# Row halves in three blocks of the output projection, and a shorter reduction at the end

## The chip, the cores and the metric

The kernel runs on one NeuronCore of a Trainium2 chip. The metric is device microseconds of one execution; the median of several executions is compared. The engines are called by the names of the profile: PE (TensorE, the matrix engine; PEld is its weight load), DVE (VectorE), ACT (ScalarE), POOL (GpSimd) and SP (SyncE, which issues most DMAs here).

## The reference

One block of a model with two branches, for 256 tokens of width 2048, with 256 context tokens beside them. The tokens are normalised and modulated, projected into many columns, go through a gated linear recurrence (16 heads) and a windowed attention (16 heads), and are merged. The change lies in the very last part:

```python
y = sigmoid(m_a + b_m[0]) * (hg_branch @ w_o_hgrn) + sigmoid(m_b + b_m[1]) * (att_branch @ w_o_attn)
h = h + gate * (y @ w_out)              # y: 256 x 2048, w_out: 2048 x 2048, gate: one row of 2048
return rmsnorm(h, final_norm_gain)      # h * rsqrt(mean(h*h) + 1e-6) * gain
```

All of it is in float32.

## The kernel before

**Products.** Every matrix is held as two parts, a high one rounded to the engine's float32r type and a low one, the rest. A product of a 128 x 128 block of activations and a 128 x 512 block of weights is three matmuls into the same bank of PSUM (`mm3`, lines 83 to 85): high x high, high x low, low x high. In the output projection the activations (`XH`, `XL`, by `y_st`) are the stationary operand, loaded by LDWEIGHTS, and the weights stream as the moving operand. The tile of activations is called `xHL` in the profile.

**Weights.** `wload` (line 66) issues the DMA of a chunk of 512 KB into one of four buffers `raw`. `wchunk` splits it: ACT copies it rounded into `wh` (line 76), DVE subtracts to get `wl` (line 77). Each of `wh` and `wl` has three buffers. Both instructions have a high priority for the scheduler, so they go ahead of other work that is ready.

**Blocks.** `proj_tok` computes 512 output columns for both token tiles (t = 0 and 1, 128 tokens each). It takes one bank for each token tile with `bank()`, from the pool `pj` of four banks, and walks over the 2048 rows of the weights two blocks of 128 at a time: a chunk gives 2 x 2 x 3 = 12 matmuls, and a block has 16 x 2 x 3 = 96. So one block uses two banks while the two of the block before are read out.

**Order.** In this stage the order of each engine is set when the program is built, by a scheduler that simulates the engines and takes the ready instruction of the highest priority. It can move products ahead of others that aren't ready yet. Semaphores keep the data right on the chip.

**The end of the kernel.** `part_b(3)`, with the last transposes of `y` (line 1061, tile `tky`) and their split, comes ahead of the output projection. Three blocks of 512 columns follow (n = 0, 1, 2), each with `settle` for both token tiles: on DVE `ht` = product x gate (line 1087) and `xv` += `ht` (line 1088), on ACT the squares and their sum (line 1091), on DVE the multiplication by the final gain (line 1096). The last 512 columns come as two pieces of 256. The first goes like a block, in chunks of 512 rows by 256 columns. For the second, all chunks are split into `bH` and `bL` (lines 884 and 885 are the lines of `split`), and its products run for token tile 0 and then for token tile 1, so that tile 0's output is finished while TensorE works on tile 1. For each tile then: `settle` of the last piece, with the squares on DVE (line 1093), a small DVE instruction that adds the sums of the other pieces (line 1127), the power -0.5 on POOL (line 1128), the scaling on ACT and DVE (lines 1132, 1135, 1137), and the output DMAs (line 1139).

Of the kernel before, what the change touches and what calls it, by code (L numbers as in the profile page):

```python
# [7 lines left out]
F32 = mybir.dt.float32  # L8
F32R = mybir.dt.float32r
U8 = mybir.dt.uint8  # L10
AF = mybir.ActivationFunctionType
ALU = mybir.AluOpType
PSUM = bass.MemoryType.PSUM

P = 128
D = 2048
T = 256
KT = D // P
# [20 lines left out]
def block_kernel(ctx: ExitStack, tc: tile.TileContext, x, c, cx, c_ctx, w_ada, b_ada, norm_gain, w_in,  # L39
                 b_merge, lb_f, lb_b, hg_gain, w_oh, sink, w_oa, w_out, fin_gain, cst, msk, out):  # L40
    nc = tc.nc
    pe, act, dve, pool = nc.tensor, nc.scalar, nc.vector, nc.gpsimd

    def pl(name, bufs=1, **kw):
        return tc.tile_pool(name=name, bufs=bufs, **kw)
# [5 lines left out]
    base = ctx.enter_context(pl("base"))  # L51
# [9 lines left out]
    def wload(w, row0, nk, col0, ncol, rp=None):  # L61

        raw = (rp or wp).tile([P, 1024], F32, tag="raw", name="raw", bufs=8 if rp else 4)
        rv = raw[:, : len(col0) * nk * ncol].rearrange("p (g k c) -> p g k c", g=len(col0), k=nk)
        for g, co in enumerate(col0):
            nc.sync.dma_start(rv[:, g], w[row0: row0 + nk * P, co: co + ncol].rearrange("(k p) c -> p k c", p=P))
        return raw, rv

    def wchunk(w, row0, nk, col0, ncol):
        cl = col0 if isinstance(col0, tuple) else (col0,)  # L70
        raw, rv = wload(w, row0, nk, cl, ncol)
        h = wp.tile([P, 1024], F32R, tag="wh", name="wh", bufs=3)
        lo = wp.tile([P, 1024], F32R, tag="wl", name="wl", bufs=3)
        n = len(cl) * nk * ncol
        with tc.high_priority(PRIO):
            act.activation(h[:, :n], raw[:, :n], AF.Copy)  # L76
            dve.tensor_tensor(lo[:, :n], raw[:, :n], h[:, :n].bitcast(F32), op=ALU.subtract)  # L77
        parts = [(h[:, g * nk * ncol: (g + 1) * nk * ncol].rearrange("p (k c) -> p k c", k=nk),
                  lo[:, g * nk * ncol: (g + 1) * nk * ncol].rearrange("p (k c) -> p k c", k=nk)) for g in range(len(cl))]
        return parts if isinstance(col0, tuple) else parts[0]  # L80

    def mm3(o, s, m, first, last):
        pe.matmul(o, s[0], m[0], start=first, stop=False)  # L83
        pe.matmul(o, s[0], m[1], start=False, stop=False)  # L84
        pe.matmul(o, s[1], m[0], start=False, stop=last)  # L85

    def bank(name="pj"):
        return pj.tile([P, 512], F32, tag="pj", name=name)

    def proj_tok_g(w, col0, src, toks):  # L90


        banks = [bank() for _ in toks]
        for k0 in range(0, KT, 2):
            h, lo = wchunk(w, k0 * P, 2, col0, 512)
            for i, t in enumerate(toks):
                for j in range(2):
                    mm3(banks[i], src(k0 + j, t), (h[:, j, :], lo[:, j, :]), k0 + j == 0, k0 + j == KT - 1)
            yield len(toks) * 6 * 512
        return banks  # L100

    def result(g):

        while True:
            try:
                next(g)
            except StopIteration as e:
                return e.value

    def proj_tok(*a):  # L110
        return result(proj_tok_g(*a))
# [109 lines left out]
    with pl("st", reuse_waits="tile") as st:  # L221
        cT = st.tile([P, KT, 32], F32, name="cT")
        mod = st.tile([P, 2, KT, 2], F32, name="mod")
        rows = st.tile([48, P], F32, name="rows")
# [8 lines left out]
        rv = lambda a: a.rearrange("(r p) -> r p", p=P)  # L233
# [649 lines left out]
    def split(dh, dl, src, **kw):  # L883
        act.activation(dh, src, AF.Copy, **kw)
        dve.tensor_tensor(dl, src, dh.bitcast(F32), op=ALU.subtract)
# [11 lines left out]
    with tc.manual_schedule(engines={mybir.EngineType.PE}):  # L897
# [25 lines left out]
        for t in range(4):  # L923
            rows = slice(8 + 2 * t, 10 + 2 * t)
# [120 lines left out]
    xv = [at.tile([P, D], F32, tag=tg, name="xv") for tg in ("A", "X2")]  # L1045
    fg = [at.tile([P, 1024], F32, tag=tg, name="fg") for tg in Q_TAGS[0]]
    gt = [at.tile([P, 1024], F32, tag=tg, name="gt") for tg in Q_TAGS[1]]
# [27 lines left out]
    def y_st(kt, t):  # L1075
        sl = slice(t * P, (t + 1) * P)
        return XH[:, kt, sl], XL[:, kt, sl]

    fin = few.tile([P, 16], F32, name="fin")
    ssf = fin[:, :10].rearrange("p (t n) -> p t n", t=2)  # L1080
    rsf = fin[:, 10:12]
    def settle(t, bo, c0, width, slot, gain=True):

        cl = slice(c0, c0 + width)
        ch = slice(c0 % 1024, c0 % 1024 + width)
        ht = base.tile([P, 512], F32, tag="bb", name="ht", bufs=2)[:, :width]
        dve.tensor_tensor(ht, bo, gt[c0 // 1024][:, ch], op=ALU.mult)
        dve.tensor_tensor(xv[t][:, cl], xv[t][:, cl], ht, op=ALU.add)
        sq = base.tile([P, 512], F32, tag="sm", name="fsq", bufs=3)[:, :width]
        if gain:  # L1090
            act.activation(sq, xv[t][:, cl], AF.Square, accum_out=ssf[:, t, slot: slot + 1])
        else:
            dve.scalar_tensor_tensor(sq, xv[t][:, cl], 1.0, xv[t][:, cl], op0=ALU.mult, op1=ALU.mult,
                                     accum_out=ssf[:, t, slot: slot + 1])
        if gain:
            dve.tensor_tensor(xv[t][:, cl], xv[t][:, cl], fg[c0 // 1024][:, ch], op=ALU.mult)

    for n in range(3):
        bo = proj_tok(w_out, n * 512, y_st, range(2))
        for t in range(2):  # L1100
            settle(t, bo[t], n * 512, 512, n)

    bo = [bank() for _ in range(2)]
# [5 lines left out]
    for k0 in range(0, KT, 4):  # L1109
        raw, _ = wload(w_out, k0 * P, 4, (D - 256,), 256)  # L1110
        rv = raw.rearrange("p (k c) -> p k c", k=4)
        ks = slice(k0, k0 + 4)
        with tc.high_priority(PRIO):
            split(bH[:, ks, :], bL[:, ks, :], rv)
    for t in range(2):
        settle(t, bo[t][:, :256], D - 512, 256, 3)

        tot = fin[:, 12 + t: 13 + t]
        dve.tensor_reduce(tot, ssf[:, t, 0:4], mybir.AxisListType.X, ALU.add)
        dve.tensor_scalar(tot, tot, 1.0 / D, EPS, op0=ALU.mult, op1=ALU.add)  # L1120
    for t in range(2):
        be = bank()
        for kt in range(KT):
            mm3(be[:, :256], y_st(kt, t), (bH[:, kt, :], bL[:, kt, :]), kt == 0, kt == KT - 1)
        settle(t, be[:, :256], D - 256, 256, 4, False)
        rs = rsf[:, t: t + 1]
        dve.tensor_scalar(rs, ssf[:, t, 4:5], 1.0 / D, fin[:, 12 + t: 13 + t], op0=ALU.mult, op1=ALU.add)
        pool.tensor_tensor(rs, rs, mhalf[:, :1], op=ALU.pow)
        for c0, c1, on_act in ((0, 512, True), (512, 1024, False), (1024, 1536, True), (1536, D, False)):
            o_ = xv[t][:, c0: c1]  # L1130
            if on_act:
                act.activation(o_, o_, AF.Copy, scale=rs)
            else:
                e = min(c1, D - 256)
                dve.tensor_scalar(xv[t][:, c0: e], xv[t][:, c0: e], rs, None, op0=ALU.mult)
                if e < c1:
                    dve.scalar_tensor_tensor(xv[t][:, e: c1], xv[t][:, e: c1], rs, fg[1][:, e - 1024: c1 - 1024],
                                             op0=ALU.mult, op1=ALU.mult)
            (nc.scalar if on_act else nc.sync).dma_start(out[t * P: (t + 1) * P, c0: c1], o_)
# [53 lines left out]
```

## Time and profile before

| what | value |
|---|---|
| median of 3 runs | 1636.76 us (1636.32 to 1637.85) |
| the profiled execution's own time | 1636.14 us |
| span of the profile, first to last instruction | 1634.3 us |
| PE, DVE, ACT busy | 99%, 57%, 47% of the span |
| mean granted PE clock | 0.997 |
| output projection, blocks of 512 columns | about 1537 to 1603 us |
| output projection, pieces of 256 columns | 1603 to 1626 us |
| behind the last matmul | 1626.3 to 1634.3 us |

Times in rows of the timeline are microseconds from the start of the span: first the start, then the duration, then engine, line, operation, and output<-inputs. `128*128` is the part of the array that a matmul uses, rows x columns, and `128x512` what it writes or streams. A row with `x2` at its end merges neighbours of one kind. Matmuls overlap in the array, so the duration of one is its latency; what a stream of them costs is read from the distance of their starts. In rows that group instructions, the numbers after the bar are the total busy time in us, the mean of one in ns, and the idle time before them with what ended it. Some matmul records are missing from a trace.

### The profile page before, as it was taken

How to read it: one execution, taken by the hardware profiler on the slowest of the kernel's cores; microseconds unless marked ns; L12 is line 12 of the kernel's file. 1: busy time of each engine (PE TensorE's matmuls, PEld its weight loads, DVE VectorE, ACT ScalarE, POOL GpSimd, SP SyncE). 2: the span in 40 equal slices, each digit the busy share in tenths (PEclk: the TensorE clock that was granted, in tenths of full speed). 3: DMA queues.
4: the chain of work that ended last, by engine and by line, in shares of the span. 5: the costliest groups of instructions: out<-in, count | busy, mean ns of one | idle time of the engine just before them, and what ended most of it. 6: DMA issues, size and time to landing. Idle time of an engine off the chain costs nothing.

```text
span 1634.3 us, 24809 instructions
## 1 busy us (share of the span) xinstructions
PE 1613.9 (99%) x9882; PEld 1329.3 (81%) x9882; DVE 937.0 (57%) x1463; ACT 763.4 (47%) x1200; POOL 31.4 (2%) x88
## 2 busy tenths in 40 slices
PE   7999999999999999999999999999999999999998
PEld 4558888888888888888888888888888888788887
DVE  4444467536665466645567455235677676555565
ACT  4333454424553345433566443224576787454443
POOL 2000000000000000000000000000000000000000
PEclk9999999999999999999999999999999999999999
DMA  9993444336343453435335555424544454665554
GB/s 356 383 384 109 142 150 149 110 127 195 104 129 117 156 176 106 131 117 177 118 119 176 186 193 193 129 90 142 179 140 146 133 168 157 231 201 192 184 191 140
DMA packets 191427, 274.89 MB, mean 168 GB/s; under 512 B 9776, under 2 KB 112592, under 8 KB 190544
## 3 DMA queue, kind: packets, MB, share of 16 engines
q1 hardware_dynamic: 189344, 268.95, 50.1%
q0 software_dynamic: 1248, 3.25, 0.7%
q8 instruction: 77, 1.26, 0.3%
q10 hardware_dynamic: 720, 1.11, 0.2%
q14 instruction: 38, 0.31, 0.1%
HBM read 271.17 MB, written 2.11 MB: 167 GB/s over the span
## 4 chain that ended last, share of the span: by engine, by line
PE 95%; DMA 2%; DVE 1%; issue 1%; ACT 0%; SPq 0%; POOLq 0%; POOL 0%; ACTq 0%
PE pj L83 24%; PE pj L85 23%; PE pj L84 23%; PE pj L141 7%; PE pj L146 4%; DMA raw<-in_w_ada_dram 2%; PE pa L306 2%; PE al L562 1%; PE pj L396 1%; PE pj L389 1%; PE sb L643 1%; PE tkp L1001 1%; PE pj L390 1%; PE oba L83 0%; PE sc L85 0%
## 5 line engine op out<-in xcount | busy, mean ns | idle before, releaser
L77 DVE TENSOR_TENSOR wl<-raw,wh 128x1024 fp32r<-128x1024 f32 x392 | 479.6, 1224 | 425.4 <-ACT wh L76 425.0
L76 ACT ACTIVATE wh<-raw 128x1024 fp32r<-128x1024 f32 x392 | 414.7, 1058 | 589.4 <-PE pj L85 428.6
L84 PE MATMUL pj<-wl,xHL 128*128 128x512 f32 (+1 forms) x1024 | 395.6, 386 | 0.4 <-DVE wl L77 0.4
L85 PE MATMUL pj<-wh,xHL 128*128 128x512 f32 (+1 forms) x1024 | 395.4, 386 | 0.0
L83 PE MATMUL pj<-wh,xHL 128*128 128x512 f32 (+1 forms) x1024 | 391.4, 390 | 0.0
L85 PEld LDWEIGHTS pj<-wh,xHL 128*128 128x128 f32 x1024 | 192.4, 188 | 39.0
L84 PEld LDWEIGHTS pj<-wl,xHL 128*128 128x128 f32 x1024 | 192.5, 188 | 38.2 <-DVE wl L77 0.7
L83 PEld LDWEIGHTS pj<-wh,xHL 128*128 128x128 f32 x1024 | 192.2, 188 | 37.8 <-DVE yt L1057 0.4
L141 PE MATMUL pj<-xHL,wh 128*128 128x512 f32 x512 | 181.1, 396 | 0.0
L83 PE MATMUL pj<-xHL,wh 128*128 128x512 f32 x416 | 164.6, 396 | 0.0
L85 PE MATMUL pj<-xHL,wl 128*128 128x512 f32 x416 | 162.1, 390 | 0.0
L84 PE MATMUL pj<-xHL,wh 128*128 128x512 f32 x416 | 162.0, 389 | 0.0
L146 PE MATMUL pj<-xHL,wl 128*128 128x256 f32 x512 | 139.9, 283 | 0.0
L141 PEld LDWEIGHTS pj<-xHL,wh 128*128 128x128 f32 x512 | 95.0, 188 | 19.2
L84 PE MATMUL pj<-wl,bH 128*128 128x512 f32 x256 | 99.9, 390 | 0.0
L85 PE MATMUL pj<-wh,bL 128*128 128x512 f32 x256 | 99.6, 389 | 0.0
L146 PEld LDWEIGHTS pj<-xHL,wl 128*128 128x128 f32 x512 | 96.7, 189 | 2.5
L85 PEld LDWEIGHTS pj<-xHL,wl 128*128 128x128 f32 x416 | 78.1, 188 | 16.7
L83 PEld LDWEIGHTS pj<-xHL,wh 128*128 128x128 f32 x416 | 78.1, 188 | 15.5
L84 PEld LDWEIGHTS pj<-xHL,wh 128*128 128x128 f32 x416 | 78.2, 188 | 15.4
L83 PE MATMUL pj<-wh,bH 128*128 128x512 f32 x256 | 89.8, 390 | 0.1
L608 DVE TENSOR_TENSOR A<-A,X 128x512 f32<-128x512 f32 x96 | 62.0, 687 | 16.7 <-ACT qk L538 6.7
(278 smaller groups left out, 1688.2 us busy)
## 6 DMA issues: line engine op xcount, KB each, us to landing
raw<-in_w_in_dram SPq DMA_DIRECT2D x292, 512.0 KB, 3.5
raw<-in_w_ada_dram SPq DMA_DIRECT2D x128, 256.0 KB, 5.5
raw<-in_w_ada_dram SPq DMA_DIRECT2D x32, 512.0 KB, 3.7
raw<-in_w_o_hgrn_dram SPq DMA_DIRECT2D x32, 512.0 KB, 3.5
raw<-in_w_o_attn_dram SPq DMA_DIRECT2D x32, 512.0 KB, 3.7
raw<-in_w_out_dram SPq DMA_DIRECT2D x32, 512.0 KB, 4.3
raw<-in_w_in_dram SPq DMA_DIRECT2D x24, 256.0 KB, 5.5
X<-in_x_dram SPq DMA_DIRECT2D x2, 1024.0 KB, 6.7
```

The costliest lines, as they stand in the source:

```text
L76: act.activation(h[:, :n], raw[:, :n], AF.Copy)
L77: dve.tensor_tensor(lo[:, :n], raw[:, :n], h[:, :n].bitcast(F32), op=ALU.subtract)
L83: pe.matmul(o, s[0], m[0], start=first, stop=False)
L84: pe.matmul(o, s[0], m[1], start=False, stop=False)
L85: pe.matmul(o, s[1], m[0], start=False, stop=last)
L141: pe.matmul(banks[i].rearrange("p (a t) -> p a t", a=2), h[:, j, cs_], xHL[:, :, kt, :T], start=kt == 0, stop=kt == KT - 1)
L146: pe.matmul(banks[i][:, :T], lo[:, j, cs_], xH[:, kt, :T], start=False, stop=False)
L306: pe.matmul(pa[32 * g: 32 * g + 32, : 2 * w], cT[:, k0 + g, :], rv_[:, :, g % nk, :], start=k0 == 0, stop=k0 == KT - 4, tile_position=(0, ...
L389: pe.matmul(o, hw, xH[:, kt, :], start=kt == 0, stop=False)
L390: pe.matmul(o, lo[:, kt - k, cs_], xH[:, kt, :], start=False, stop=False)
L396: pe.matmul(o, hw, xL[:, kt, :], start=False, stop=kt == KT - 1)
L608: dve.tensor_tensor(av, av, f.unsqueeze(3).to_broadcast([P, 2, n2, b]), op=ALU.mult)
```

## The change

Three edits, all behind `part_b`.

- In the three blocks of 512 columns, `proj_tok` is replaced by the new `in_rows`. It takes four banks, two for each token tile. Each of the three matmuls of a product becomes two: one over the upper 64 rows of the array (partitions 0 to 63 of both operands) into one bank, one over the lower 64 rows into the other. At the end of the block ACT copies the second bank into SBUF and DVE adds the first.
- In the last 256 columns the gate is multiplied into the weights, four times 128 x 1024 on DVE before the split, in place of a multiplication of each product.
- In the last chain of each token tile the product is added to `xv` straight from PSUM, and the squares, their sum, the factor 1/D and the sum of the other pieces are one DVE instruction.

```diff
-    def settle(t, bo, c0, width, slot, gain=True):
+    def settle(t, bo, c0, width, slot):
...
-        if gain:
-            act.activation(sq, xv[t][:, cl], AF.Square, accum_out=ssf[:, t, slot: slot + 1])
-        else:
-            dve.scalar_tensor_tensor(sq, xv[t][:, cl], 1.0, xv[t][:, cl], op0=ALU.mult, op1=ALU.mult,
-                                     accum_out=ssf[:, t, slot: slot + 1])
-        if gain:
-            dve.tensor_tensor(xv[t][:, cl], xv[t][:, cl], fg[c0 // 1024][:, ch], op=ALU.mult)
+        act.activation(sq, xv[t][:, cl], AF.Square, accum_out=ssf[:, t, slot: slot + 1])
+        dve.tensor_tensor(xv[t][:, cl], xv[t][:, cl], fg[c0 // 1024][:, ch], op=ALU.mult)
+
+    def in_rows(col0):
+
+        banks = [[bank(), bank()] for _ in range(2)]
+        for k0 in range(0, KT, 2):
+            m = wchunk(w_out, k0 * P, 2, col0, 512)
+            for t in range(2):
+                for j in range(2):
+                    s = y_st(k0 + j, t)
+                    for n_, (a, b) in enumerate(((0, 0), (0, 1), (1, 0))):
+                        for r in range(2):
+                            rows = slice(64 * r, 64 * r + 64)
+                            pe.matmul(banks[t][r], s[a][rows], m[b][rows, j, :], start=k0 + j + n_ == 0,
+                                      stop=k0 + j == KT - 1 and n_ == 2, tile_position=(64 * r, 0))
+        out_ = []
+        for t in range(2):
+            o = base.tile([P, 512], F32, tag="sm", name="rsum", bufs=3)
+            act.activation(o, banks[t][1], AF.Copy)
+            dve.tensor_tensor(o, banks[t][0], o, op=ALU.add)
+            out_.append(o)
+        return out_
 
     for n in range(3):
-        bo = proj_tok(w_out, n * 512, y_st, range(2))
+        bo = in_rows(n * 512)
         for t in range(2):
             settle(t, bo[t], n * 512, 512, n)
...
         with tc.high_priority(PRIO):
+
+            dve.tensor_tensor(rv, rv, gt[1][:, 768:].unsqueeze(1).to_broadcast([P, 4, 256]), op=ALU.mult)
             split(bH[:, ks, :], bL[:, ks, :], rv)
...
-        settle(t, be[:, :256], D - 256, 256, 4, False)
         rs = rsf[:, t: t + 1]
-        dve.tensor_scalar(rs, ssf[:, t, 4:5], 1.0 / D, fin[:, 12 + t: 13 + t], op0=ALU.mult, op1=ALU.add)
+        xe = xv[t][:, D - 256:]
+        dve.tensor_tensor(xe, xe, be[:, :256], op=ALU.add)
+        sq = base.tile([P, 512], F32, tag="sm", name="fsq", bufs=3)[:, :256]
+        dve.tensor_tensor_reduce(sq, xe, xe, 1.0 / D, fin[:, 12 + t: 13 + t], op0=ALU.mult, op1=ALU.add, accum_out=rs)
         pool.tensor_tensor(rs, rs, mhalf[:, :1], op=ALU.pow)
```

## The prediction

> **What bounds the kernel now.** I read the page first (busy shares and the chain that ended last), then the windows over the output projection, then the timeline of single engines at the places that the diff touches.
>
> ```profile
> span 1634.3 us, 24809 instructions
> ...
> PE 1613.9 (99%) x9882; PEld 1329.3 (81%) x9882; DVE 937.0 (57%) x1463; ACT 763.4 (47%) x1200; POOL 31.4 (2%) x88
> ...
> PE 95%; DMA 2%; DVE 1%; issue 1%; ACT 0%; SPq 0%; POOLq 0%; POOL 0%; ACTq 0%
> ```
>
> TensorE is busy 99% of the span and carries 95% of the chain: a product that gets cheaper or dearer moves the end by the same amount, unless TensorE then waits. The windows show the output projection:
>
> ```profile
> 1537.00:1603.00 66.00, 66.00 (x297) 54.62 (x296) 39.62 (x43) 29.23 (x34) 0.00 (x0) 1.00 0.57 190
> 1603.00:1616.50 13.50, 13.50 (x114) 13.46 (x113) 10.54 (x13) 7.36 (x10) 0.00 (x0) 1.00 0.38 122
> ```
>
> The columns are the window, its length, then busy time of PE, PEld, DVE, ACT and POOL, granted clock, DMA share and GB/s. The first row holds the three quarters that the change rewrites (about 288 products and 8 transposes): TensorE has no idle time at full granted clock, and DVE and ACT have 26 and 37 us to spare. In the second, the first half of the last quarter, DVE is already busy 10.54 of 13.50 us.
>
> Next is the price of a product. The first two rows stand 12 products of 512 columns apart, the last two 45 products of 256 columns:
>
> ```profile
> 1578.64 0.62 PE L83 MATMUL pj<-wh,xHL 128*128 128x512 f32 x2
> ...
> 1581.36 0.62 PE L83 MATMUL pj<-wh,xHL 128*128 128x512 f32 x2
> ...
> 1620.63 0.28 PE L85 MATMUL pj<-bH,xHL 128*128 128x256 f32 x1
> ...
> 1626.03 0.28 PE L85 MATMUL pj<-bH,xHL 128*128 128x256 f32 x1
> ```
>
> 2.72 / 12 = 226.7 ns and 5.40 / 45 = 120.0 ns. The difference of 106.7 ns over 256 columns is 0.417 ns a column, so 512 columns stream in 213.4 ns and each product carries 13.3 ns beside the streaming. That 13.3 ns is all that halves running together can take away.
>
> **The change part by part. The halves (term A).** 3 x 16 x 2 x 3 = 288 products become 576 matmuls of 64 rows, each still streaming 512 columns. If two halves run together with nothing beside the streaming, a pair costs 213.4 ns: 288 x -13.3 = -3.8 us. If they run one after the other it costs 2 x 226.7: +65.3 us. No row of this trace shows row halves. The nearest are tiles of 32 array columns, against the same kind of matmul untiled:
>
> ```profile
> 234.02 0.39 PE L85 MATMUL pj<-xHL,wl 128*128 128x512 f32 x1
> 234.34 0.46 PE L562 MATMUL al<-Kmt 128*32 128x32 f32 x32
> ...
> 235.21 0.65 PE L562 MATMUL al<-so,acc 128*32 128x64 f32 x32
> 235.80 0.66 PE L669 MATMUL kt<-cs,A 128*128 128x128 f32 x4
> ...
> 245.69 0.39 PE L702 MATMUL ob<-so,A 128*128 128x128 f32 x2
> ...
> 246.36 0.39 PE L702 MATMUL ob<-so,A 128*128 128x128 f32 x2
> ```
>
> Untiled, six matmuls of 128 columns lie between the last two rows: 112 ns each, 0.87 ns a column, so 64 columns would take some 56 ns. The 32 tiled ones of 64 columns start within 0.65 - 0.22 = 0.43 us (0.22 us is one's latency), 14 ns each, so four take 56 ns: four column tiles run in the time of one, and their weight loads with them. I carry that over to row halves, with the weight loads as the doubt:
>
> ```profile
> L84 PEld LDWEIGHTS pj<-wl,xHL 128*128 128x128 f32 x1024 | 192.5, 188 | 38.2 <-DVE wl L77 0.7
> ...
> L562 PEld LDWEIGHTS al<-acc,Kmt 128*32 128x32 f32 x256 | 3.1, 108 | 0.0
> ...
> L1061 PEld LDWEIGHTS tky<-cs,y 128*128 128x128 f32 x32 | 4.0, 139 | 1.0
> ...
> L1061 PE MATMUL tky<-cs,y 128*128 128x128 f32 x32 | 4.8, 272 | 0.0
> ...
> 1542.77 0.60 PE L1061 MATMUL tky<-cs,y 128*128 128x128 f32 x4
> ...
> L349 PEld LDWEIGHTS tp<-cs,rows 80*128 80x128 f32 x1 | 0.1, 143 | 0.0
> ```
>
> A load goes by columns: 188 - 108 = 80 ns for 96 more is 0.83 ns a column, 107 ns for 128; and 80 rows (143 ns) cost what 128 rows do (139 ns, the same operation). So a half's load is no cheaper, and a pair has two: 2 x 107 = 213 ns if they take turns, just what the streaming takes. The closest that matmuls with a load of 128 columns each stand in this trace is 109 ns (the four transposes at 1542.77: 0.60 less one's 0.27 leaves 0.33 for three) to 120 ns (the 256-column products), so taking turns gives 218 to 240 ns. I take 219 ns, between 213.4 and the first of these: 288 x -7.7 = -2.2 us. Ends of the likely case -3.8 and 0.
>
> [...]
>
> **The banks (term B).** The pool pj has four banks. Before, a block takes two and the next block has the other two; now a block takes all four, and the next one must wait until ACT has copied each upper half and DVE has added the lower.
>
> ```profile
> 1580.00 0.39 PE L85 MATMUL pj<-wh,xHL 128*128 128x512 f32 x1
> ...
> 1581.13 0.39 PE L85 MATMUL pj<-wh,xHL 128*128 128x512 f32 x1
> ...
> 1579.93 1.23 DVE L77 TENSOR_TENSOR wl<-raw,wh 128x1024 fp32r<-128x1024 f32 x1 [1.49 <-ACT wh L76]
> 1581.08 1.28 DVE L1087 TENSOR_TENSOR ht<-pj,gt 128x512 f32<-128x512 f32 x2
> ...
> 1581.56 1.06 ACT L76 ACTIVATE wh<-raw 128x1024 fp32r<-128x1024 f32 x1 [1.66 <-PE pj L85]
> ...
> L884 ACT ACTIVATE xHL<-tky 128x512 fp32r<-128x512 f32 x4 | 2.4, 590 | 1.9 <-PE tky L1061 1.9
> ```
>
> These are the last products of token tiles 0 and 1 in the second block. Tile 0 ends at 1580.39; the copy (0.59) is done near 1581.0, but DVE is in L77 until 1581.1, so the sum (0.68 by L1087's two in 1.28) frees the first bank near 1581.8, while TensorE wants it at 1581.36: 0.43 us of waiting. Tile 1 ends at 1581.52. Copied before L76 its banks come free at 1582.9, ahead of the 1583.2 when TensorE gets there (0.43 late, six products). Copied behind L76 (1581.56 + 1.06), which is put ahead, the sum ends at 1584 to 1584.5: 0.7 to 1.4 us more. Queued behind these waits on ACT and DVE are only the next chunk's splits, which run up to three chunks ahead. Two boundaries at 0.43 to 1.8 us, and the third (the last quarter wants two banks, both of tile 0) at 0.43: 1.3 to 4.0. The order is the scheduler's and fits TensorE's next ready matmuls into part of it: I take 1.8.
>
> **Switching (term C).** Into the tiled stretch above there are 0.32 us from L85 to L562 where 0.23 is usual (+0.09), out of it 0.16 (235.64 to 235.80) in place of 0.01 (+0.15): 0.24 a round trip. The stage is entered and left once, and two groups of part_b's transposes (the first at 1542.77, above) fall into its start: up to three round trips, 0.7. I take 0.6, between 0 (transposes placed ahead, drain covered) and 0.9.
>
> **The end (term D).**
>
> ```profile
> 1626.35 0.42 DVE L1087 TENSOR_TENSOR ht<-pj,gt 128x256 f32<-128x256 f32 x1 [2.32 <-PE pj L85]
> 1626.81 0.42 DVE L1088 TENSOR_TENSOR xv<-xv,ht 128x256 f32<-128x256 f32 x1
> 1627.27 0.42 DVE L1093 SCALAR_TENSOR_TENSOR fsq<-xv 128x256 f32<-128x256 f32 x1
> 1627.62 0.08 DVE L1093 DVE_READ_ACCUMULATOR fsq<-xv 128x1 f32 x1
> 1627.73 0.21 DVE L1127 TENSOR_SCALAR fin<-fin 128x1 f32<-128x1 f32 x1
> 1628.03 0.56 POOL L1128 TENSOR_TENSOR fin<-fin,mhalf 128x1 f32<-128x1 f32 x1 [5.18 <-DVE fin L1127]
> 1628.62 1.33 ACT L1132 ACTIVATE xv<-xv,fin 128x512 f32<-128x512 f32 x2 [4.40 <-POOL fin L1128]
> ```
>
> Token tile 1's last chain lies bare behind TensorE. The gate multiplication goes (1626.81 - 1626.35 = 0.46) and L1127 goes into the reduction (1628.03 - 1627.73 = 0.30): -0.76. The fused multiply-and-reduce has no row here; at 0 to 0.3 us over L1093's 0.42 the gain is 0.76 to 0.46. I take -0.7. Tile 0's copy of it lies under TensorE.
>
> **The gate moved into the weights (term E).** The same gate now multiplies four chunks of raw weights on DVE, ahead of their split:
>
> ```profile
> 1614.16 1.06 ACT L884 ACTIVATE bH<-raw 128x1024 fp32r<-128x1024 f32 x1 [2.66 <-DMA raw<-in_w_out_dram]
> ...
> 1615.25 1.23 DVE L885 TENSOR_TENSOR bL<-raw,bH 128x1024 fp32r<-128x1024 f32 x1 [2.00 <-ACT bH L884]
> ```
>
> Four at 1.23 (L885's size) are 4.9 us, and the two new sums 1.3: 6.2 us into a window where DVE has 3.0 idle and some 2.7 of settle's work that can be put off. The last chunk is ready at 1616.5 now; TensorE needs it for tile 0's last 12 products, at 1620.6 - 12 x 0.12 = 1619.1, so 2.6 us of cover. The chain from its DMA's landing grows by 1.2 us, and the buffer that this DMA waits for comes free later by what DVE is behind, another 1 to 2. Cost 0 to 2 us; I take 0.5.
>
> **Sum**: -2.2 + 1.8 + 0.6 - 0.7 + 0.5 = 0.0 us. The profiled execution took 1636.14 us (span 1634.3 and 1.8 around it), the median run 1636.76; I forecast the median, 1636.8.
>
> **The rivals.** (1) Full overlap and mild waits: A = -3.8, B = 0.9 (0.43 at each boundary, partly filled), C = 0.2, D = -0.76, E = 0: -3.5 us, 1633.3. For it: the four column tiles. Against: each of the five terms must fall near its good end.
>
> (2) Slower by one mechanism: the two loads of a pair take turns, and each stands as far from the next as 256-column products do, 120 ns. A pair then costs 240 ns, A = 288 x 13.3 = +3.8 and the sum +6.0: 1642.8. It costs more than it saves from 227 ns a pair on. For it: a load goes by columns. Against: the 109 ns of transposes, and the column tiles' loads, which do overlap.
>
> (3) Overlap as forecast, but both banks' sums are queued behind the splits at both inner boundaries (B = 4.0) and the gated chunks come late (E = 2): +3.7, 1640.5. DVE's window of 10.54 in 13.50 speaks for it, the slack of 2.6 us against.
>
> (4) The change doesn't do what it says: halves run one after the other, +65.3, about 1702. Against it stand the tiled rows at 234 to 235 us; but those are column tiles.
> [...]
>
> **How the numbers follow.** Forecast 0.54, rival 1 0.15, rival 2 0.13, rival 3 0.11, rival 4 0.07. A measurement of this kernel tells about 0.2%, 3.3 us, from no change. Rival 1 is faster (0.15); rivals 2 to 4 slower (0.31); the forecast is within. The likeliest case alone: -3.8 + 1.3 - 0.7 = -3.2 to 0 + 2.5 + 0.9 - 0.5 + 0.5 = +3.4, so 1633.6 to 1640.2. The range reaches to rivals 1 to 3 and leaves out 4 and the far tails: 1633.0 to 1643.0.
>
> **What would show it.** Starts of matmul pairs in the three blocks 213 to 227 ns apart, both halves within some 20 ns of each other; TensorE gaps of 0.4 us or more at the three block boundaries, released by DVE's sum; POOL's last start some 1.0 us behind TensorE's end in place of 1.7. Pairs over 227 ns apart, or TensorE idle on the gated chunks around 1617 to 1620 us, would make the prediction wrong.

## The result and the profile after

The changed kernel takes 1648.32 us (median of 4 runs, 1647.78 to 1648.35) against 1636.89 us before (4 runs): 1.0067 times the time, 95% interval 1.0055 to 1.0079, or 9.0 to 12.9 us slower. The forecast of 1636.8 us (1633.0 to 1643.0) was wrong. The profiled execution took 1648.35 us, 2 us around its span. First the page, which answers to the three lines shown of before:

```profile
span 1646.4 us, 25398 instructions
...
PE 1621.2 (98%) x10170; PEld 1335.8 (81%) x10170; DVE 944.8 (57%) x1469; ACT 766.7 (47%) x1206; POOL 31.1 (2%) x88
...
PE 92%; DMA 6%; DVE 1%; issue 1%; ACT 0%; SPq 0%; POOLq 0%; POOL 0%; DVEq 0%; ACTq 0%
```

PE has 288 instructions more and 98% in place of 99%. Most of the larger DMA share lies in the weights at the start of the kernel (w_ada has 4% in the list by line) and isn't the change's. Where the time went is told by windows over the three stages: from part_b's last products to the first product of 256 columns; from there to the last product; from there to the end. Before, then after:

```profile
1536.41:1603.12 66.71, 66.71 (x299) 55.21 (x298) 40.33 (x44) 29.23 (x34) 0.00 (x0) 1.00 0.57 191
1603.12:1626.03 22.91, 22.91 (x192) 22.91 (x191) 15.67 (x30) 9.72 (x16) 0.57 (x1) 1.00 0.30 101
1626.03:1634.34 8.31, 0.28 (x3) 0.08 (x1) 2.64 (x8) 1.33 (x2) 0.56 (x1) 0.67 0.46 171
```

```profile
1537.69:1613.73 76.04, 71.45 (x587) 59.55 (x585) 45.06 (x49) 33.25 (x41) 0.00 (x0) 0.99 0.51 169
1613.73:1638.80 25.07, 25.07 (x192) 25.07 (x192) 19.66 (x33) 9.32 (x16) 0.57 (x1) 0.91 0.28 93
1638.80:1646.41 7.61, 0.27 (x3) 0.07 (x1) 2.06 (x6) 1.33 (x2) 0.56 (x1) 0.73 0.49 182
```

The second column is the length. The three blocks grew by 9.33 us, 4.59 of them with PE idle (76.04 - 71.45); the last quarter by 2.16, at a mean granted clock of 0.91; the end shrank by 0.70. These three sum to 10.8 us, while the two spans differ by 12.1: the stage also began 1.28 us later in the profiled execution of after, ahead of everything that the diff touches. 0.9 of it is PE time lost in the first 130 us of the kernel (117.66 us busy against 118.58). That start moves between 1536.5 and 1538.1 over the kernels below (e5, with halves, 1536.5; e7, without, 1536.9); with one profile of each, whether the change has a part in it stays open.

**The pairs.** Two rows of the timeline of after, twelve pairs apart, then the group of their weight loads and a pair of them:

```profile
1575.13 0.40 PE L1104 MATMUL pj<-wh,xHL 64*128 64x512 f32 x2
...
1577.85 0.40 PE L1104 MATMUL pj<-wh,xHL 64*128 64x512 f32 x2
```

```profile
L1104 PEld LDWEIGHTS pj<-wh,xHL 64*128 64x128 f32 x384 | 45.0, 184 | 7.3 <-issue 0.7
...
1575.36 0.20 PEld L1104 LDWEIGHTS pj<-wl,xHL 64*128 64x128 f32 x2
```

Two halves last 0.40 us together and one 0.39, so they run at the same time; so do their loads, two in 0.20 us at 0.184 each. But 2.72 us for twelve pairs is 226.7 ns, exactly the full product's distance. The 13.3 ns beside the streaming is still there.

**The inner boundaries.** Windows of 8 us of after, one inside a block and two over the boundaries, and rows from the first boundary:

```profile
1570.00:1578.00 8.00, 8.00 (x74) 6.89 (x72) 4.34 (x4) 3.30 (x4) 0.00 (x0) 1.00 0.61 190
1560.00:1568.00 8.00, 8.00 (x61) 6.83 (x58) 6.84 (x9) 3.86 (x7) 0.00 (x0) 1.00 0.57 198
1582.00:1590.00 8.00, 8.00 (x60) 6.90 (x57) 6.44 (x9) 3.93 (x6) 0.00 (x0) 1.00 0.54 189
```

```profile
1562.23 0.61 PE L1104 MATMUL pj<-wh,xHL 64*128 64x512 f32 x2
1562.68 0.39 PE L1104 MATMUL pj<-wl,xHL 64*128 64x512 f32 x1
1562.91 0.61 PE L1104 MATMUL pj<-wh,xHL 64*128 64x512 f32 x2
```

PE is never idle there, yet 13 and 14 halves fewer go through: at 113 ns each (half a pair's distance) 1.5 and 1.6 us lost. The rows show why: three halves take 0.68 us (1562.23 to 1562.91), 227 ns each. They run alone, and a lone half costs what a pair costs. That it is because the bank of the other half isn't free is borne out by the runs with more banks below (e4 and e8), in which most of this goes.

**The third boundary.** PE, ACT and DVE of after, each from its own timeline:

```profile
1613.73 0.58 PE L83 MATMUL pj<-wh,xHL 128*128 128x256 f32 x1 [4.59 <-ACT rsum L1109]
```

```profile
1606.46 1.06 ACT L76 ACTIVATE wh<-raw 128x1024 fp32r<-128x1024 f32 x1 [1.66 <-PE pj L1104]
1612.14 1.06 ACT L884 ACTIVATE bH<-raw 128x1024 fp32r<-128x1024 f32 x1 [4.62 <-DVE raw L1131]
1613.10 0.58 ACT L1109 ACTIVATE rsum<-pj 128x512 f32<-128x512 f32 x1
```

```profile
1604.83 1.23 DVE L77 TENSOR_TENSOR wl<-raw,wh 128x1024 fp32r<-128x1024 f32 x1 [1.49 <-ACT wh L76]
1610.88 1.23 DVE L1131 TENSOR_TENSOR raw<-raw,gt 128x1024 f32<-128x1024 f32 x1 [4.82 <-DMA raw<-in_w_out_dram]
```

The transfer in the chain of waits, and a window behind the gap (the 0.50 is the granted clock):

```profile
1606.09 4.67 DMA raw<-in_w_out_dram
```

```profile
1613.73:1618.00 4.27, 4.27 (x20) 4.27 (x21) 3.93 (x6) 2.11 (x4) 0.00 (x0) 0.50 0.68 213
```

PE waits 4.59 us for ACT's copy of a bank (L1109); some expectations below count this gap from other points, 4.7 to 5 us. The copy itself takes 0.58 us, and its products were done before 1609.2; but in ACT's row it stands behind the split of a chunk of the last piece (L884), that one waits for the new gate product on DVE (L1131), and that for a transfer which only began at 1606.09, when DVE's L77 had freed its buffer. Then 20 products run at a granted clock of 0.50, 213 ns apart in place of 120: 1.9 us more; the distance falls back to 0.12 us near 1618.4. So 4.59 us of waiting was followed by some 4.6 us at half clock (for a shorter wait see e5).

**The end.** Its chain in after, from the last product (1638.80) on:

```profile
1639.57 0.48 DVE L1147 CUSTOM_DVE_ANT_0 fsq<-xv,fin 128x256 f32<-128x256 f32 x1
1639.98 0.08 DVE L1147 DVE_READ_ACCUMULATOR2_ANT fin<- 128x1 f32 x1
...
1640.73 1.33 ACT L1152 ACTIVATE xv<-xv,fin 128x512 f32<-128x512 f32 x2 [3.80 <-POOL fin L1148]
```

1640.73 - 1638.80 = 1.93 us against 2.59 before (1628.62 - 1626.03): -0.66. The fused reduction takes 0.06 us more than the plain one (0.48 against 0.42).

### The profile page after: what moved, and what is told of

It reads as the page before. It is cut to its first block, busy times and chain, and to the rows that moved or that the text cites. A ratio compares the mean times of both kernels' runs of the same rounds, so it can differ in the third digit from the quotient of the medians.

```text
span 1646.4 us, 25398 instructions
## 1 busy us (share of the span) xinstructions
PE 1621.2 (98%) x10170; PEld 1335.8 (81%) x10170; DVE 944.8 (57%) x1469; ACT 766.7 (47%) x1206; POOL 31.1 (2%) x88
## 4 chain that ended last, share of the span: by engine, by line
PE 92%; DMA 6%; DVE 1%; issue 1%; ACT 0%; SPq 0%; POOLq 0%; POOL 0%; DVEq 0%; ACTq 0%
PE pj L83 22%; PE pj L85 22%; PE pj L84 22%; PE pj L141 7%; DMA raw<-in_w_ada_dram 4%; PE pj L1104 4%; PE pj L146 4%; PE al L562 1%; PE sb L643 1%; PE tkp L1001 1%; DMA raw<-in_w_in_dram 1%; PE pa L306 1%; PE pj L396 1%; PE oba L83 0%; DMA X<-in_x_dram 0%
## 5 line engine op out<-in xcount | busy, mean ns | idle before, releaser
L77 DVE TENSOR_TENSOR wl<-raw,wh 128x1024 fp32r<-128x1024 f32 x392 | 479.1, 1223 | 420.7 <-ACT wh L76 420.1
L76 ACT ACTIVATE wh<-raw 128x1024 fp32r<-128x1024 f32 x392 | 414.7, 1058 | 581.2 <-PE pj L85 395.0
L83 PE MATMUL pj<-wh,xHL 128*128 128x512 f32 (+1 forms) x928 | 359.3, 391 | 4.6 <-ACT rsum L1109 4.6
L84 PE MATMUL pj<-wl,xHL 128*128 128x512 f32 (+1 forms) x928 | 359.1, 387 | 0.4 <-DVE wl L77 0.4
L85 PE MATMUL pj<-wh,xHL 128*128 128x512 f32 (+1 forms) x928 | 358.8, 387 | 0.0
L83 PEld LDWEIGHTS pj<-wh,xHL 128*128 128x128 f32 x928 | 175.3, 189 | 39.1 <-ACT rsum L1109 5.0
L85 PEld LDWEIGHTS pj<-wh,xHL 128*128 128x128 f32 x928 | 175.1, 189 | 35.5
L84 PEld LDWEIGHTS pj<-wl,xHL 128*128 128x128 f32 x928 | 175.6, 189 | 34.5 <-DVE wl L77 0.7
```

## The experiments

All were timed in 5 rounds beside the kernel before on the same chip: medians of before 1636.73, 1636.22 and 1636.67 us in the three groups. All but the first keep the shorter end; diffs are against the changed kernel, those of the last two groups against the group before them.

**Row halves alone** (e1): the gate and the end as before.

```diff
-            dve.tensor_tensor(rv, rv, gt[1][:, 768:]..., op=ALU.mult)
...
+        settle(t, be[:, :256], D - 256, 256, 4, False)
+        dve.tensor_scalar(rs, ssf[:, t, 4:5], 1.0 / D, fin[:, 12 + t: 13 + t], op0=ALU.mult, op1=ALU.add)
```

> Only the row halves are kept; the gate goes back into settle and the last chain is that of before. Theory 1 (halves gain nothing, and TensorE loses at the three block boundaries because a block holds all four banks and the copies that free them queue on ACT): pairs stay at 227 ns, about 3.2 us lost at the two inner boundaries, and at the third a TensorE gap still above 3 us, since the copy stands behind the split of the first chunk of the last piece (L884), which waits for its DMA with or without the gate; 9 to 13 us slower than before. Theory 2 (the gate multiplication on DVE delays the last quarter, and the banks cost only the inner boundaries): the gap at the third boundary is below 1 us and the kernel 4 to 6 us slower than before.

1647.37 us, 1.0062 (1.0050 to 1.0075). Two of its waits at the third boundary (in all, number, longest):

```profile
ACT bH L884 <- DMA raw<-in_w_out_dram: 9.5, 2, 5.8
...
PE pj L83 <- ACT rsum L1114: 4.0, 1, 4.0
```

Without the gate product ACT's split waits for the transfer itself, and PE stands for 4.0 us. So the halves, with the banks that they take, and not the gate product, carry nearly all of the loss.

**The end alone** (e2): full-row products in the three blocks.

```diff
-        bo = in_rows(n * 512)
+        bo = proj_tok(w_out, n * 512, y_st, range(2))
```

> The three blocks are products over 128 rows again, in two banks; the gate in the last weights and the fused reduction stay. Theory 1: TensorE has no gap over 0.5 us, the last chain is some 0.6 us shorter, and the kernel is 0 to 0.8 us faster than before. Theory 2: the four multiplications of 1.23 us on DVE make the last chunks late, TensorE idles 2 to 6 us between 1603 and 1620 us, and the kernel is 2 to 6 us slower than before.

1637.69 us, 1.0006 (0.9997 to 1.0015): no gain. Its last window, and two rows of DVE in it:

```profile
1626.48:1636.03 9.55, 0.28 (x3) 0.07 (x1) 3.11 (x9) 2.67 (x4) 0.56 (x2) 0.69 0.60 221
```

```profile
1626.52 0.75 DVE L1155 TENSOR_SCALAR xv<-xv,fin 128x512 f32<-128x512 f32 x2 [0.69 <-POOL fin L1148]
...
1627.58 0.41 DVE L1145 TENSOR_TENSOR xv<-xv,pj 128x256 f32<-128x256 f32 x1
```

The stage behind the last product is 9.55 us long in place of 8.31. Tile 0's last chain begins at 1624.88 in place of 1620.59; since PE has no gap, the scheduler must have mixed its last products with those of tile 1 (PE's rows don't name the tile). So tile 0 is only scaled at 1626.52, when tile 1's products are done, and tile 1's chain begins behind it, 1.1 us behind the last product in place of 0.3. That takes back what the shorter chain gains (tile 1 is scaled 2.71 us behind the last product, 2.59 before); the rest lies in the outputs, which leave 2.7 us apart in place of 5.7, so that all of their 2.1 MB move behind the last product.

**The last piece loaded early on SP's queue** (e3), into four buffers that this stage doesn't need.

```diff
-        raw, _ = wload(w_out, k0 * P, 4, (D - 256,), 256)
+        raw = fp.tile([P, 2, 512], F32, tag=("F0", "F0", "F1", "acc")[k0 // 4], ...)
+        nc.sync.dma_start(rv, w_out[k0 * P: (k0 + 4) * P, D - 256: D]...)
```

> The changed kernel, with the four chunks of the last piece loaded into four buffers that are free by then instead of the shared raw buffers, so that their DMAs, gate multiplications and splits lie in the three blocks, ahead of the third boundary. Theory 1: the copies at the third boundary no longer stand behind a split that waits for a DMA; the gap of 5 us shrinks to below 1.5 us and the stretch at half clock behind it disappears: 4 to 6 us faster than the changed kernel, still 4 to 7 us slower than before, for the inner boundaries stay. If the copies themselves are what is slow, the gap stays and the time is the changed kernel's within 1.5 us.

1647.28 us, 1.0064 (1.0051 to 1.0076). The gap at the third boundary is gone, and one nearly as long has come some 60 us earlier. From its chain of waits:

```profile
1539.78 1.21 DVE yt L1057 x2
1541.01 4.76 DMA raw<-in_w_out_dram
...
1549.28 0.69 DVE xHL L885
...
1550.02 1.11 PE tky L1061 x4
```

The scheduler took the chance to put the gate products and splits early too, ahead of the split of y that PE's next transposes wait for; one of their transfers came late, since its buffer came free only with part_b's last products on DVE (L1057), and PE stood 3.9 us at the transposes. The loss follows the late transfer.

**Eight banks** (e4): the second block and the last quarter take four banks of the attention's pool.

```diff
+    def other(i):
+        return ps.tile([P, 512], F32, tag=("al1", "al2", "o", "tp")[i], name="pother")
...
-        banks = [[bank(), bank()] for _ in range(2)]
+        banks = [[other(2 * t + r) if col0 == 512 else bank() for r in range(2)] for t in range(2)]
...
-    bo = [bank() for _ in range(2)]
+    bo = [other(t) for t in range(2)]
...
-        be = bank()
+        be = other(2 + t)
```

> The changed kernel, with the second block and the last quarter in the four other banks of PSUM, which are idle by then; the other blocks keep the four of the pool. Nothing waits for a copy now. Theory 1: the excess at the inner boundaries (3.2 us) and the gap at the third (4.7 us and the half clock) go; a wait of up to 2 us for a late chunk may take the place of the last: 0 to 4 us slower than before. If row halves are slow by themselves, it stays 7 us or more slower than before.

1645.44 us, 1.0050 (1.0036 to 1.0063). Most of the loss at the inner boundaries goes (395 halves in place of 372 between 1560 and 1605 us) and no product waits for a bank at the third. But PE then waits for weights instead, by its chain:

```profile
1602.30 4.63 DMA raw<-in_w_out_dram
...
1609.44 5.22 DMA raw<-in_w_out_dram
...
1615.83 1.23 DVE wl L77
...
1617.10 0.58 PE pother L84
```

The same late gate product stands in DVE's row ahead of the next chunks' L77. Each L77 frees the buffer of the next transfer, so two transfers of some 5 us come one after the other, and the half clock follows (0.53 from 1617.10 to 1622.50). Banks are not the cause of the long gap; they were only the first thing that ran out behind it.

**The last piece on GpSimd's queue** (e5, four banks; e6, eight banks; e7, full-row products): as e3, with the loads taken out of SP's row.

```diff
-        nc.sync.dma_start(rv, w_out[k0 * P: (k0 + 4) * P, D - 256: D]...)
+        nc.gpsimd.dma_start(rv, w_out[k0 * P: (k0 + 4) * P, D - 256: D]...)
```

> The changed kernel, except that the four chunks of the last piece are loaded by GpSimd's DMA queue, early, into buffers that nothing uses any more, so that neither their gate products nor their splits wait for a transfer in SyncE's row. Theory (the 4.98 us gap at the third boundary comes from ScalarE and VectorE standing in order behind work that waits for the late transfer): the gap falls below 1.5 us and the products at half clock behind it go; left are about 0.9 us of mode changes, 3.2 us at the two inner boundaries, 0.5 to 1.5 us at the third and -0.6 us at the end, 1640.7 to 1642 us in all. Rival (the gap is the price of freeing four banks at that boundary, whatever waits behind): the gap stays above 3 us and the time at 1646 to 1649 us.

> As the kernel with the loads on GpSimd's queue, and the second block and the last quarter take four other banks, so that no boundary waits for a bank. Theory (a pair of halves costs what a full product costs, 226.7 ns, and all the loss is at boundaries and in waits): 0.9 us of mode changes, 0.3 to 0.8 us left at the boundaries, -0.6 us at the end, and any gate product that is late: 1637 to 1639 us. Rival (the pairs themselves cost more than full products): 1641 us or more without a gap in TensorE's row.

> The same early loads on GpSimd's queue and the shorter end chain, but full-row products in the three blocks. Theory: with no late transfer the two token tiles end one after the other again, about 5.7 us apart, the shorter chain shows, and the time is 1635.9 to 1636.8 us. Rival (the early loads disturb the stage before as much as they help, by crowding the transfers of the other weights): 1637.5 us or more, with new waits for transfers between 1500 and 1560 us. Against the kernel with eight banks it gives the price of the halves alone: the theory says 0.8 to 2 us, the rival that pairs are dearer says 4 us or more.

e5: 1645.37 us, 1.0053 (1.0041 to 1.0066). e6: 1642.70, 1.0037 (1.0023 to 1.0051). e7: 1636.14, 1.0000 (0.9991 to 1.0008). The third boundary behaved as the theory said (no gap, no half clock), but the first two missed their times by 3.4 and 3.7 us: the last of the four buffers comes free late, and its gate product was again placed ahead of the split of y. In e5 that wait, and the windows behind it:

```profile
PE tky L1061 <- DVE xHL L885: 2.4, 1, 2.4
```

```profile
1549.30:1553.00 3.70, 3.70 (x20) 2.94 (x22) 2.34 (x4) 1.63 (x2) 0.00 (x0) 0.54 0.50 149
1553.00:1556.00 3.00, 3.00 (x30) 2.54 (x28) 0.98 (x1) 1.03 (x1) 0.00 (x0) 1.00 0.70 226
```

2.4 us of waiting and nearly 3.7 us at about half clock, some 1.7 us more. In e7, with full-row products, PE has no gap.

**The last piece's work given a late place** (e9, four banks; e8, eight banks; e10, full-row products): loads as in e5, and a product of one element by zero ties each chunk's gate product and split to a chunk of the second or third block. They also lose the high priority that they have in the changed kernel.

```diff
+    def last_piece(q, after_):
+        dve.scalar_tensor_tensor(rv[:, 0, :1], after_, 0.0, rv[:, 0, :1], op0=ALU.mult, op1=ALU.add)
+        dve.tensor_tensor(rv, rv, gt[1][:, 768:]..., op=ALU.mult)
+        split(bH[:, ks, :], bL[:, ks, :], rv)
...
             m = wchunk(w_out, k0 * P, 2, col0, 512)
+            if col0 and k0 in (4, 10):
+                last_piece((2 if col0 == 1024 else 0) + (k0 == 10), m[1][:, 0, :1].bitcast(F32))
...
-        with tc.high_priority(PRIO):
...
-            split(bH[:, ks, :], bL[:, ks, :], rv)
```

> The changed kernel with the last piece's four chunks loaded early by GpSimd's queue, and their gate products and splits tied to two chunks each of the second and third block (a product of one element by zero from that chunk is added first), so that in ScalarE's and VectorE's rows they stand at a place where their data landed long before. Theory (of the 11.4 us lost, some 7 us is engines standing in order behind a late transfer and the half clock after it): no gap above 1 us and no products at half clock in the output projection; 0.9 us of mode changes, 3.2 us at the inner boundaries, 0.3 to 1 us at the third, -0.65 us at the end: 1639.9 to 1641.5 us. Rival (four banks freed at once stall TensorE by themselves at the third boundary): a gap of over 3 us there, 1643 us or more.

> The same, and the second block and the last quarter take four other banks. Theory: 0.9 us of mode changes, 0.3 to 0.8 us at the inner boundaries, -0.65 us at the end: 1636.8 to 1638.2 us, with every pair at 226.7 ns. Rival (the pairs are dearer than full products by themselves): 1640 us or more without a gap.

> The same placing of the last piece's work and the shorter end chain, with full-row products in the three blocks. Theory: TensorE's row has no gap, the end chain is 0.65 us shorter: 1635.6 to 1636.6 us; against the kernel with eight banks it gives the price of the halves alone, 0.8 to 2 us. Rival (the end gains nothing, because the output's transfers set it): 1636.2 us, within 0.1% of before, with the tail after the last product still at 8.1 to 8.3 us.

e9: 1641.62 us, 1.0028 (1.0017 to 1.0039), just above its range. e8: 1638.08, 1.0008 (0.9999 to 1.0016). e10: 1636.14, 0.9997 (0.9988 to 1.0006). The three stages of e9, e8 and e10:

```profile
1537.64:1609.45 71.81, 71.81 (x587) 60.75 (x586) 52.70 (x60) 35.44 (x43) 0.75 (x1) 1.00 0.53 178
1609.45:1632.46 23.01, 23.01 (x193) 23.01 (x192) 11.83 (x26) 6.42 (x13) 0.57 (x1) 1.00 0.12 43
1632.46:1640.29 7.83, 0.28 (x3) 0.07 (x1) 2.06 (x6) 1.33 (x2) 0.56 (x1) 0.66 0.39 147
```

```profile
1537.36:1605.94 68.58, 68.53 (x588) 54.86 (x586) 52.16 (x60) 35.45 (x43) 0.75 (x1) 1.00 0.56 186
1605.94:1628.95 23.01, 23.01 (x194) 23.01 (x192) 11.83 (x26) 6.41 (x13) 0.57 (x1) 1.00 0.12 44
```

```profile
1536.53:1603.23 66.70, 66.70 (x299) 55.23 (x298) 50.01 (x56) 33.50 (x38) 0.75 (x1) 1.00 0.57 191
...
1626.14:1634.02 7.88, 0.28 (x3) 0.08 (x1) 2.06 (x6) 1.33 (x2) 0.56 (x1) 0.79 0.40 147
```

With four banks and row halves as in the change, PE is now busy through, and the clock stays at 1.00 even in the last quarter. So after - e9 (11.4 - 5.0 = 6.5 us, each against the kernel before beside it; 4.23 + 2.06 in the first two stages) is the price of standing behind the late transfer. e9 - e8 (3.54 of medians, 3.23 in the first stage) is the price of four banks at the inner boundaries. e8 - e10 (1.94 of medians, 1.88 + 0.10 in the stages) is what halves cost by themselves. None of these kernels is measurably faster than before: the end chain is shorter in e10 (8.31 to 7.88 us for the stage), but 0.4 us is below what the runs can tell.

## Why the prediction was wrong, point by point

**The halves (A): mis-sized.** That both halves run together held, loads included. It was carried over from column tiles by weak rows, though: their untiled 112 ns is also close to the 107 ns that the prediction gives one load of 128 columns, so it need not be the streaming. The step that failed is "I take 219 ns": of the 13.3 ns that could go, nothing went. 226.7 ns a pair makes A 0, not -2.2; that was the upper bound of the likely case. Rivals 1 (213.4 ns), 2 (240 ns) and 4 (one after the other) fall with it; rival 4's 1702 also left out the other terms (65.3 + 2.2 us would give 1704). Why the 13.3 ns stays no run tells.

**The banks (B): the step that failed and cost most.** For the third boundary I wrote 0.43 us, and that "queued behind these waits on ACT and DVE are only the next chunk's splits". I asked who waits behind the banks' sums; of what the sums themselves stand behind I asked only for one copy of the next chunk (L76), at the inner boundaries. In before, ACT already waited for such a transfer at the third boundary. Term E showed a later row of the same kind (1614.16, 2.66 us of waiting) and used it only for its slack; this one I had not used:

```profile
1604.58 1.06 ACT L884 ACTIVATE bH<-raw 128x1024 fp32r<-128x1024 f32 x1 [2.92 <-DMA raw<-in_w_out_dram]
```

It cost nothing (PE has no idle time in the windows of before above), because the last quarter's first products didn't need ACT for a bank: a block held two of the four, and DVE read them out. The change makes PE need ACT at just that place. In ACT's row the copy (1613.10) stands behind a split (1612.14) that had waited 4.62 us, though the copy's own products were done before 1609.2. The gap cost 4.6 us, and the half clock behind it 1.9 to 2.1, which no term held. e9 shows both gone, with the same four banks. Rival 3 had the family right (sums behind splits) but the wrong splits and the wrong place: those of the next chunks, at the inner boundaries.

At the inner boundaries the price was 3.1 us (1.5 + 1.6), within the bounds of 0.9 to 3.6 for two, by another form than forecast: no idle PE, but halves that run alone. That the second bank comes free with the copy and the first only with the sum would explain which halves run first; the rows don't name the half.

**Switching (C)**: 0.6 taken. That the array drains at a switch, as "drain covered" at the lower bound supposes, no run shows; the rows show later starts, 0.92 us in place of 0.67. PE's transposes of y, among the products of before (the second product behind them; the prediction shows the transposes at 1542.77) and among the pairs of after:

```profile
1543.44 0.39 PE L85 MATMUL pj<-wh,xHL 128*128 128x512 f32 x1
```

```profile
1541.65 0.66 PE L1061 MATMUL tky<-cs,y 128*128 128x128 f32 x4
1542.24 0.50 PE L1104 MATMUL pj<-wh,xHL 64*128 64x512 f32 x2
1542.57 0.39 PE L1104 MATMUL pj<-wl,xHL 64*128 64x512 f32 x2
```

From the first transpose to the second pair 0.92 us, before 0.67 to the second product (1542.77 to a product at 1543.44). Two such groups at 0.25, with about 0.09 more ahead of each, and an entry and an exit at some 0.1 to 0.2 make some 1.0 us, an estimate from these rows; e8's 1.88 us leaves 0.9 for its two inner boundaries.

**The end (D)** came at -0.66 in the chain, -0.7 forecast. That it shows at the end of the kernel was taken for granted: in e2 the order of the last products took it back.

**The gate in the weights (E)**: after and e1 are too near each other for their times to tell (intervals of 1.0055 to 1.0079 and 1.0050 to 1.0075). By the stages of the two profiles the gate product cost 1.1 us, within its 0 to 2: 0.56 in the first (76.04 against 75.48) as a longer chain in front of the copy (4.59 against 4.0 us of waiting), not as late chunks, and 0.57 in the second (25.07 against 24.50), where the half clock lasts longer. In e9 and e10 it costs nothing that the stages show.

**The sum by the runs**: 0 + 3.1 + 4.6 + 2.1 + 1.0 - 0.7 = 10.1 us against 10.8 in the three stages and 11.4 of the medians (9.0 to 12.9); E's longer wait is in the 4.6. Some of the rest is unpaired halves at the end of the third block (1608.08 to 1608.76), of which the profile shows 0.3 us.

**The signs named.** Pairs 226.7 ns apart with both halves together came as said, and so did POOL's last start, 1.06 us behind PE's end (1640.14 against 1638.80 + 0.28). Neither sign against the prediction came, and it was wrong all the same: PE's gap lay at 1609 to 1614, not at 1617 to 1620, and it was released by ACT's copy, not by DVE's sum.

**Open**: why the scheduler puts the last piece's first split ahead of the copies. The split and the gate product carry the high priority (`tc.high_priority(PRIO)`, line 1129), the copies and sums of `in_rows` have none; that alone would do it, if on the scheduler's clock the transfer has landed by then. It would land early on that clock if a half is counted at a full product's price. Neither was tried: no run gives the copies the same priority, and e9 changes the priority and the place of the splits together.

## What to carry to other kernels

When a change makes the bounding engine wait for an engine that was off the path, read that engine's row in order at this place, and look for the nearest instruction ahead that waits for a transfer: a wait that was harmless before is then on the path, and on TensorE the idle stretches of 2.4 us (e5) and 4.6 us (after) were each followed by a stretch at half clock, which cost some 1.7 and 1.9 us more. Splitting a full-height product into row halves gains nothing here, a pair costs what the product costs (226.7 ns), and an unpaired half costs as much (227 ns); the banks and the sums come on top. When a stall moves under an experiment (third boundary, then the transposes, then the weights), follow the late transfer and not the resource that ran out.

## What the runs showed of the hardware

- Two matmuls of 64 rows and 512 columns on both halves of the array run together and take 226.7 ns a pair, no less than one of 128 rows; one alone takes 227 ns (rows of after).
- Their loads of 64 x 128 take 184 ns each, two of them 0.20 us together (after).
- The half clock followed 2.4 us of waiting in e5 and lasted nearly 3.7 us (0.54 in the window); it followed 4.5 us in e4 (0.53 in the next 5.40 us) and 4.59 us in after (0.50). The other wait of e4, 0.9 us (5.4 us in two waits, the longer 4.5), did not bring it (1.00 in the next 2.93 us).
